# The shortest chunk of tokens first, and the attention statistics in the order of the tokens

## The chip, the cores and the metric

The kernel runs on one core of one Trainium2 chip. The metric is the device time of one launch in microseconds (us). The engines of the core are TensorE (PE, matrix products and transposes), VectorE (DVE), ScalarE (ACT), GpSimd (POOL), and SyncE (SP), which here only issues DMAs.

## The reference

One decoder layer for 1024 tokens of a prompt and 8 single tokens of other sequences, all in fp32. What matters here:

```python
h = rms_norm(x, norm_mix_pre)
q, k, v, u, gates = jnp.split(h @ w_in, IN_SPLITS, axis=-1)
...
# three groups of 4 heads, each with its own dilation (1, 4, 16); one log-sum-exp per token, head, group
w = jax.nn.softmax(jnp.stack(lses, axis=0), axis=0)
o = jnp.einsum('gbth,gbthd->bthd', w, jnp.stack(outs, axis=0))
...
a, gte = jnp.split(u, 2, axis=-1)
z = a * jax.nn.sigmoid(gte)        # then a causal depthwise convolution of width 31, and so on
```

Behind them come the merge of both branches, the output projection, a SwiGLU feed-forward and a per-layer embedding, each with an RMSNorm. The change doesn't touch these.

## The kernel before

The 1032 tokens are the free axis of all activations, features lie on the 128 partitions, so a tensor of 1024 features is 8 pieces of 128 x 1032. For matmuls the tokens go in three chunks, `CH`: 0 to 383, 384 to 767, and 768 to 1031 (264 tokens, the 8 single ones among them). Every fp32 product is done as three matmuls on split operands (L278 to L280): high weight by high activation, high weight by low activation, low weight by high activation. `hh` and `hl` are the high and low parts of the normed input, `wh` and `wl` those of a weight of 8 x 128 x 128, whose raw form (`raw`) is loaded from DRAM, split by ACT (`wh`) and by DVE (`wl`). `gemm_bank` computes one bank of PSUM: 8 pieces of k, so 24 matmuls, for one weight and one chunk.

`first_pairs` is the start of the program. Nothing is normed yet, so the first two chunks that it takes are multiplied unnormed ("plain"), each token's factor being applied later to the product (`u_evac` multiplies by `rbx`, sigmoid, multiplies again; `a_evac` multiplies into `z`). Meanwhile the factors are made: `norm_sums` squares on ACT and adds on DVE (tiles `sq`, `acc`), `token_rstd` transposes the sums on PE (L325), reduces on DVE (`cs`), and raises to the power -1/2 on POOL (`r`); `bcast_cols` spreads the factor back over the partitions with three transposes on PE (L337). The third chunk is normed properly before it is multiplied (`norm_apply`: a scaling `hf` on DVE, `hh` on ACT, `hl` on DVE, for each of 8 pieces), and the first two are normed afterwards for all later weights. Each engine takes its work in order; what the order is, is decided when the program is built, by a scheduler that mostly keeps the written order of `first_pairs` on ACT and DVE but lets PE's banks run in turn.

Attention runs in the order that suits each group's dilation. Each (token, head, group) has two statistics (maximum and sum), collected in `stats[g]` (tiles `st`) by blocks of the group's order. `stats_by_tokens(g)` writes them over DRAM (`d_st`) and reads them back so that partition and column are a token's, with POOL issuing the DMAs. From them `combine` makes one factor for each token, head and group, sends it to DRAM and reads it broadcast over 64 partitions (`fb`), and multiplies the groups' outputs (`ogl`, 128 x 1024, two heads of a group) by it: three multiplies and two adds for each of two pairs of heads, all on DVE, between other work (the feed-forward has not begun; the norm of the convolution and its products run on PE, and other sums of squares, tiles `acc` and `sq`, stand on DVE and ACT).

Of the kernel before, what the change touches and what calls it, by code (L numbers as in the profile page):

```python
# [12 lines left out]
AF = mybir.ActivationFunctionType  # L13
# [3 lines left out]
P = 128  # L17
S = 1024
# [3 lines left out]
KT = D // P  # L22
# [5 lines left out]
CH = ((0, 384), (384, 384), (768, 264))  # L28
CW = 384
# [29 lines left out]
def decoder_step(ctx: ExitStack, tc: tile.TileContext, ins, outs):  # L59
# [30 lines left out]
    def rl(s):  # L90
        return rlp.tile([P, CW], F32, tag="rl", name=nm(s))
# [332 lines left out]
    xin = {}  # L424

    def vec(v, f):
        return vecs[:, v, f:f + 1]

    def load_x(c):
        xin[c] = chunk_slots("xin")  # L430
        load_chunk(xin[c][0], xT_in, c)

    hs = [(act("hh", F32R), act("hl", F32R)) for _ in range(KT)]
    rbx = [rl("rb0"), rl("rb1")]

    def load_raw(n):
        while w_emitted[0] < n:
# [7 lines left out]

    def norm_factor(r1, c):
        rb = bcast_cols(r1, c)
        A.activation(rbx[c], rb[:, :CW], AF.Copy)

    def norm_apply(c, fs, rb):  # L450
        t0, n = CH[c]
# [10 lines left out]
            last = (hf, f)  # L462

    def norm_plain(c, f):
        split_scaled(xin[c][1][f], vec(V_MIXPRE, f), hs[f][0], hs[f][1], c)


    def setup():
# [115 lines left out]

    def stats_by_tokens(g):

        dst, src = stats[g], d_st[g]
        G.dma_start(src, stats[g])
        if g == 0:
            for b in range(8):  # L590
                G.dma_start(dst[b * 16:(b + 1) * 16], src[:, b].rearrange("(p b) n -> p b n", b=8))
        elif g == 1:
            for l in range(2):
                for e in range(2):
                    G.dma_start(dst[l * 64:(l + 1) * 64, e * 4:(e + 1) * 4],
                                 src[e::2, l::2])
        else:
            for j in range(2):
                for i in range(2):
                    G.dma_start(dst[j::2, i * 4:(i + 1) * 4],  # L600
                                 src[i * 64:(i + 1) * 64, j * 4:(j + 1) * 4])

    class Unit:

# [152 lines left out]
    def triple_bank(i, j, c):  # L757
        g, hp = triples[i]
        t0, n = CH[c]
        if c == 0:  # L760
# [110 lines left out]
    def combine(beside):  # L871
# [48 lines left out]
        for _ in range(W2):  # L920
            yield next(beside)
        for hp in range(2):
            ovs = [o[:, :S].rearrange("p (t b) -> p b t", b=8) for o in o3]
            for g in range(3):
                V.tensor_mul(ovs[g], ovs[g], f3[g][:, :S].rearrange("p (b t) -> p b t", b=8))
                yield 1.2
                if g:
                    V.tensor_add(o3[0][:, :S], o3[0][:, :S], o3[g][:, :S])
                    yield 1.2
            V.tensor_copy(o3[0][:, S:T], osm[:, hp])  # L930
            o = o3[0]
# [15 lines left out]
    def u_evac(i, c, sig, ps, rb=None):  # L947
        n = CH[c][1]
        s = rl("sg")
        if rb is not None:  # L950
            V.tensor_mul(s, ps[:, :n], rb)
            A.activation(s, s, AF.Sigmoid)
            V.tensor_mul(s, s, rb)
        else:
            A.activation(s[:, :n], ps[:, :n], AF.Sigmoid)
        sig[i, c] = s

    def a_evac(i, c, sig, zs, ps):
        t0, n = CH[c]
        if c == 0:  # L960
# [6 lines left out]
        if c < 2:  # L967
            return
        V.tensor_mul(t38, ps[:, 226:264], s[:, 226:264])
# [32 lines left out]
    def first_pairs():  # L1002

        nonlocal gtags, mtags
        mtags, gtags = deque(MT0), deque(GT0)
        sig, zs = {}, {}  # L1010
        pinned[0] = True
        A.activation(mhalf2, mhalf, AF.Sigmoid)
        xin[0] = chunk_slots("xin")
        SY.dma_start(vecs, ins["vecs"])
        load_chunk(xin[0][0][:1], xT_in, 0)
        load_raw(1)
        load_chunk(xin[0][0], xT_in, 0, 1)
        load_raw(3)
        load_x(1)
        for f in range(2):  # L1020
            norm_plain(0, f)
        ensure(0)
        for f in range(2, KT):
            norm_plain(0, f)
        g0 = gemm_bank(wi_gate[0], hs, 0)
        load_raw(4)
        load_x(2)
        SY.dma_start(cc, ins["cc"])
        SY.dma_start(taps, ins["taps"])
        ensure(2)  # L1030
        a0 = gemm_bank(wi_a[0], hs, 0)
        t = norm_sums(0)
        for f in range(3):
            norm_plain(1, f)
        r1 = token_rstd(t, 0)
        ensure(3)
        for f in range(3, 6):
            norm_plain(1, f)
        g1 = gemm_bank(wi_gate[1], hs, 0, mid=lambda: norm_factor(r1, 0), at=KT - 1)
        u_evac(0, 0, sig, g0, rbx[0])  # L1040
        a_evac(0, 0, sig, zs, a0)
        for f in range(6, KT):
            norm_plain(1, f)
        t = norm_sums(1)
        u_evac(1, 0, sig, g1, rbx[0])
        a1 = gemm_bank(wi_a[1], hs, 0)
        r1 = token_rstd(t, 1)
        t = norm_sums(2)
        a_evac(1, 0, sig, zs, a1)
        g0 = gemm_bank(wi_gate[0], hs, 1, mid=lambda: norm_factor(r1, 1))  # L1050
        r2 = token_rstd(t, 2)
        u_evac(0, 1, sig, g0, rbx[1])
        rb = []
        a0 = gemm_bank(wi_a[0], hs, 1, mid=lambda: rb.append(bcast_cols(r2, 2)))
        norm_apply(2, range(2), rb[0])
        a_evac(0, 1, sig, zs, a0)
        g1 = gemm_bank(wi_gate[1], hs, 1)
        norm_apply(2, range(2, KT), rb[0])
        u_evac(1, 1, sig, g1, rbx[1])
        a1 = gemm_bank(wi_a[1], hs, 1)  # L1060
        norm_apply(0, range(3), rbx[0])
        a_evac(1, 1, sig, zs, a1)
        ensure(4)
        for i in range(2):
            u_evac(i, 2, sig, gemm_bank(wi_gate[i], hs, 2))
            norm_apply(0, range(3 + 3 * i, 6 + 2 * i), rbx[0])
            a_evac(i, 2, sig, zs, gemm_bank(wi_a[i], hs, 2))
            ensure(wi_a[1] + 2 + i)
        norm_apply(1, range(KT), rbx[1])
        xin.clear()  # L1070
        pinned[0] = False
        mtags, gtags = deque(["m"]), deque(["g"])

    def triple(i):
        for j in range(3):
            for c in (0, 2, 1) if i == 0 and j == 0 else range(3):
# [584 lines left out]
```

## Time and profile before

| | before |
|---|---|
| median of 3 runs | 1696.8 us (1696.02 to 1697.6) |
| profiled execution, its own time | 1694.75 us |
| its span in the trace | 1693.0 us |
| PE busy | 1675.4 us (99% of the span) |
| DVE busy | 1201.1 us (71%) |
| ACT busy | 610.6 us (36%) |
| granted TensorE clock, mean | 1.00 |

The span is the time from the first to the last instruction of the profiled execution; the run's own time has 1.75 us more around it. Times of single instructions below come from this one execution. Matmuls are pipelined, so the busy time of one in a row is longer than the distance to the next.

### The profile page before, as it was taken

The page shows a single profiled execution, that of the slowest core. Times are in us where ns is not written, and L with a number is a line of the kernel's source. Part 1 is how long each engine was busy: PE and PEld are TensorE (multiplying, and loading weights), DVE is VectorE, ACT ScalarE, POOL GpSimd, SP SyncE. Part 2 cuts the span into 40 slices and gives each one's busy share as a digit, 9 for nine tenths or more (in the row PEclk, how much of TensorE's full clock was granted, in tenths as well). Part 3 has the DMA queues.
Part 4 walks back from the last instruction along what each step waited for, and adds up shares of the span by engine and source line. Part 5 has one row for each costly group of instructions (what it writes and reads, how often), then busy time and mean ns, then how long its engine had stood idle before and what let it go on. Part 6 is the DMA issues. An engine that isn't in the chain of part 4 may idle for free.

```text
span 1693.0 us, 28665 instructions
## 1 busy us (share of the span) xinstructions
PE 1675.4 (99%) x11651; PEld 1648.9 (97%) x11651; DVE 1201.1 (71%) x2084; ACT 610.6 (36%) x1231; POOL 29.2 (2%) x46
## 2 busy tenths in 40 slices
PE   8999999999999999999999999999999999999999
PEld 7999999999999999999999999999999999999998
DVE  7899879958979686553679666666666445548863
ACT  6434435444343345123444323323323311213520
POOL 1000010000000000000000000000000000000000
PEclk9999999999999999999999999999999999999999
DMA  5242121121354364423232222323333523420411
GB/s 191 65 125 66 44 69 57 50 82 51 102 177 159 93 191 128 147 73 120 85 124 82 81 99 88 101 86 114 110 107 125 185 109 114 162 96 14 159 51 47
DMA packets 81307, 174.72 MB, mean 103 GB/s; under 512 B 11491, under 2 KB 50291, under 8 KB 80791
## 3 DMA queue, kind: packets, MB, share of 16 engines
q1 hardware_dynamic: 80566, 172.69, 31.2%
q8 instruction: 91, 1.49, 0.4%
q0 software_dynamic: 608, 0.20, 0.1%
q14 instruction: 42, 0.34, 0.1%
HBM read 136.20 MB, written 50.16 MB: 110 GB/s over the span
## 4 chain that ended last, share of the span: by engine, by line
PE 91%; DVE 5%; issue 1%; ACT 1%; DMA 1%; POOL 0%; SPq 0%; POOLq 0%; DVEq 0%; ACTq 0%
PE g L278 29%; PE g L280 29%; PE g L279 29%; DVE y L120 3%; PE O L677 1%; PE S L632 1%; PE PT L659 1%; DVE wl L120 1%; DVE ogl L120 0%; DVE acc L120 0%; PE m L337 0%; DMA res<-d_x 0%; PE m L325 0%; POOL r L120 0%; DMA raw<-in_w_in_dram 0%
## 5 line engine op out<-in xcount | busy, mean ns | idle before, releaser
L278 PE MATMUL g<-hh,wh 128*128 128x384 f32 (+1 forms) x1200 | 392.9, 327 | 7.1 <-ACT wh L120 7.1
L280 PE MATMUL g<-hh,wl 128*128 128x384 f32 (+1 forms) x1200 | 384.2, 320 | 0.2 <-DVE wl L120 0.2
L279 PE MATMUL g<-hl,wh 128*128 128x384 f32 (+1 forms) x1200 | 383.7, 320 | 0.0
L120 DVE SCALAR_TENSOR_TENSOR y<-z,taps,y 128x1023 f32<-128x1023 f32 (+14 forms) x240 | 303.9, 1267 | 36.7 <-ACT y L120 31.1
L278 PEld LDWEIGHTS g<-hh,wh 128*128 128x128 f32 x1200 | 226.4, 189 | 14.4 <-ACT wh L120 7.0
L279 PEld LDWEIGHTS g<-hl,wh 128*128 128x128 f32 x1200 | 226.2, 188 | 0.6 <-DVE hl L120 0.3
L280 PEld LDWEIGHTS g<-hh,wl 128*128 128x128 f32 x1200 | 225.7, 188 | 0.8 <-DVE wl L120 0.8
L280 PE MATMUL g<-uh,wl 128*128 128x344 f32 x528 | 168.7, 320 | 0.0
L279 PE MATMUL g<-ul,wh 128*128 128x344 f32 x528 | 168.5, 320 | 0.0
L278 PE MATMUL g<-uh,wh 128*128 128x344 f32 x528 | 163.1, 321 | 0.6 <-DVE fa L120 0.6
L120 DVE TENSOR_TENSOR wl<-raw,wh 128x1024 fp32r<-128x1024 f32 x106 | 129.1, 1221 | 35.3 <-ACT wh L120 28.6
L120 DVE TENSOR_TENSOR pk<-pk,g 128x258 f32<-128x258 f32 x266 | 105.4, 420 | 55.0 <-PE g L280 39.0
L120 ACT ACTIVATE wh<-raw 128x1024 fp32r<-128x1024 f32 x106 | 110.7, 1051 | 6.9 <-PE g L279 3.8
L278 PE MATMUL g<-mh,wh 128*128 128x344 f32 x336 | 107.3, 322 | 0.0
L280 PE MATMUL g<-mh,wl 128*128 128x344 f32 x336 | 107.1, 320 | 0.0
L279 PE MATMUL g<-ml,wh 128*128 128x344 f32 x336 | 107.0, 320 | 0.0
L120 DVE TENSOR_TENSOR fa<-fa,g 128x344 f32<-128x344 f32 x96 | 47.1, 510 | 77.2 <-PE g L280 76.8
L279 PEld LDWEIGHTS g<-ul,wh 128*128 128x128 f32 x528 | 99.3, 188 | 0.0
L280 PEld LDWEIGHTS g<-uh,wl 128*128 128x128 f32 x528 | 99.2, 188 | 0.0
L278 PEld LDWEIGHTS g<-uh,wh 128*128 128x128 f32 x528 | 98.0, 188 | 0.9 <-DVE fa L120 0.9
L278 PE MATMUL g<-th,wbh 128*128 128x258 f32 x304 | 86.0, 283 | 0.0
L280 PE MATMUL g<-th,wbl 128*128 128x258 f32 x304 | 85.9, 283 | 0.0
(234 smaller groups left out, 3700.3 us busy)
## 6 DMA issues: line engine op xcount, KB each, us to landing
raw<-in_w_in_dram SPq DMA_DIRECT2D x50, 512.0 KB
raw<-in_w_ffn_in_dram SPq DMA_DIRECT2D x44, 512.0 KB
hr<-d_h SPq DMA_DIRECT2D x22, 516.0 KB
raw<-in_w_ffn_out_dram SPq DMA_DIRECT2D x22, 512.0 KB
d_h<-pk SPq DMA_DIRECT2D x38, 258.0 KB
out_kvs_dram<-in_cache_kv_w_dram SPq DMA_DIRECT2D x16, 510.0 KB
d_x<-mo SPq DMA_DIRECT2D x24, 172.0 KB
out_yT_dram<-fa SPq DMA_DIRECT2D x24, 172.0 KB
```

The lines of the kernel that those rows point to most:

```text
L120: ins = fn(*a, **k)
L278: TE.matmul(ps, hi_w, xh, start=first, stop=False)
L279: TE.matmul(ps, hi_w, xl, start=False, stop=False)
L280: TE.matmul(ps, lo_w, xh, start=False, stop=last)
L632: TE.matmul(sp[h][:, o:o + nk], qT[h * 64:(h + 1) * 64, blk * P:(blk + 1) * P], kT[h * 64:(h + 1) * 64, (blk + 1) * P - nk:(blk + 1) * P], ...
L659: TE.transpose(ps[:, o:o + P], e[:, o:o + P], ident)
L677: TE.matmul(ps[h * 64:(h + 1) * 64, i * P:(i + 1) * P], vtok[:, k0:k0 + 64], self.p[half][:, o:o + P], start=kb == kbs[0], stop=kb == kbs[-1])
```

## The change

Three things are changed. First, `first_pairs` takes the chunks in another order: the chunk of 264 tokens first, then tokens 0 to 383, both plain, and tokens 384 to 767 last, with the norm ahead of the product; the factors `rbx` are now kept for chunks 2 and 0 and sliced to the chunk's width, and the transposes that end a pair of `z` run when its third chunk is done, whichever that is. Second, `stats_by_tokens` no longer turns the statistics into an order of 8 successive tokens on a partition: group 0 is left as it is, groups 1 and 2 are written to DRAM in two permuting DMAs (pieces of 32 and of 128 bytes) so that a row is a token, and read back by one DMA in blocks of 128 tokens. Third, the factor `fb` comes out in the tokens' order, so the multiplies in `combine` need no view that permutes. The first triple's first weight takes its chunks in the order 2, 1, 0 instead of 0, 2, 1.

```diff
-    rbx = [rl("rb0"), rl("rb1")]
+    rbx = {0: rl("rb0"), 2: rl("rb2")}
...
     def stats_by_tokens(g):
 
-        dst, src = stats[g], d_st[g]
-        G.dma_start(src, stats[g])
         if g == 0:
-            for b in range(8):
-                G.dma_start(dst[b * 16:(b + 1) * 16], src[:, b].rearrange("(p b) n -> p b n", b=8))
-        elif g == 1:
+            return
+
+        rows = d_st[g].rearrange("p b n -> (p b) n")
+        if g == 1:
+            to = rows.rearrange("(l i r) n -> l i r n", l=2, r=4)
             for l in range(2):
-                for e in range(2):
-                    G.dma_start(dst[l * 64:(l + 1) * 64, e * 4:(e + 1) * 4],
-                                 src[e::2, l::2])
+                G.dma_start(to[l], stats[1][:, l::2])
         else:
-            for j in range(2):
-                for i in range(2):
-                    G.dma_start(dst[j::2, i * 4:(i + 1) * 4],
-                                 src[i * 64:(i + 1) * 64, j * 4:(j + 1) * 4])
+            to = rows.rearrange("(l j i r) n -> i l j r n", j=2, i=2, r=4)
+            for i in range(2):
+                G.dma_start(to[i], stats[2][i * 64:(i + 1) * 64].rearrange("p (j r) n -> p j r n", j=2))
+        G.dma_start(stats[g], rows.rearrange("(b p) n -> p b n", p=P))
...
         for hp in range(2):
-            ovs = [o[:, :S].rearrange("p (t b) -> p b t", b=8) for o in o3]
             for g in range(3):
-                V.tensor_mul(ovs[g], ovs[g], f3[g][:, :S].rearrange("p (b t) -> p b t", b=8))
+                V.tensor_mul(o3[g][:, :S], o3[g][:, :S], f3[g][:, :S])
                 yield 1.2
...
+        CA, CB, CC = 2, 0, 1
...
-        load_chunk(xin[0][0][:1], xT_in, 0)
+        load_chunk(xin[CA][0][:1], xT_in, CA)
         load_raw(1)
-        load_chunk(xin[0][0], xT_in, 0, 1)
+        load_chunk(xin[CA][0], xT_in, CA, 1)
         load_raw(3)
-        load_x(1)
+        load_x(CB)
...
-        g1 = gemm_bank(wi_gate[1], hs, 0, mid=lambda: norm_factor(r1, 0), at=KT - 1)
-        u_evac(0, 0, sig, g0, rbx[0])
-        a_evac(0, 0, sig, zs, a0)
+        g1 = gemm_bank(wi_gate[1], hs, CA, mid=lambda: norm_factor(r1, CA), at=KT - 1)
+        u_evac(0, CA, sig, g0, rbx[CA])
+        a_evac(0, CA, sig, zs, a0)
...
-            u_evac(i, 2, sig, gemm_bank(wi_gate[i], hs, 2))
-            norm_apply(0, range(3 + 3 * i, 6 + 2 * i), rbx[0])
-            a_evac(i, 2, sig, zs, gemm_bank(wi_a[i], hs, 2))
+            u_evac(i, CC, sig, gemm_bank(wi_gate[i], hs, CC))
+            norm_apply(CA, range(3 + 3 * i, 6 + 2 * i), rbx[CA])
+            a_evac(i, CC, sig, zs, gemm_bank(wi_a[i], hs, CC))
             ensure(wi_a[1] + 2 + i)
-        norm_apply(1, range(KT), rbx[1])
+        norm_apply(CB, range(KT), rbx[CB])
```

On PE, around the first factor (the transposes L337 into `m_320`), the program before has these rows; `g_298` is the third bank, of the third weight, on the first chunk, and the end of a name counts the buffers.

```order
L278 MATMUL g_298<-hh_122,wh_218 128x384
L279 MATMUL g_298<-hl_123,wh_218 128x384
L280 MATMUL g_298<-hh_122,wl_219 128x384
L278 MATMUL g_298<-hh_124,wh_218 128x384
L279 MATMUL g_298<-hl_125,wh_218 128x384
L280 MATMUL g_298<-hh_124,wl_219 128x384
L337 MATMUL m_320<-ident,r_55_284 128x128 x3
L278 MATMUL g_298<-hh_126,wh_218 128x384
L279 MATMUL g_298<-hl_127,wh_218 128x384
```

After the change PE has at this place, where `g_367` is the fourth bank of the first chunk and `g_429` the first bank of the second chunk:

```order
L278 MATMUL g_298<-hh_126,wh_218 128x264
L279 MATMUL g_298<-hl_127,wh_218 128x264
L280 MATMUL g_298<-hh_126,wl_219 128x264
L278 MATMUL g_367<-hh_112,wh_288 128x264
L279 MATMUL g_367<-hl_113,wh_288 128x264
L337 MATMUL m_320<-ident,r_55_284 128x128 x3
L278 MATMUL g_429<-hh_112,wh_159 128x384
L279 MATMUL g_429<-hl_113,wh_159 128x384
L280 MATMUL g_429<-hh_112,wl_160 128x384
L278 MATMUL g_429<-hh_114,wh_159 128x384
L280 MATMUL g_367<-hh_112,wl_289 128x264
```

The factor's transposes moved behind the end of the third bank and two matmuls of the fourth: ahead of them stood 69 matmuls of 384 columns, and stand 74 of 264.

Also on PE, early in the third chunk of the start, the program before runs straight through its first bank (`g_606`):

```order
L280 MATMUL g_606<-hh_116,wl_160 128x264
L278 MATMUL g_606<-hh_118,wh_159 128x264
L279 MATMUL g_606<-hl_119,wh_159 128x264
L280 MATMUL g_606<-hh_118,wl_160 128x264
L278 MATMUL g_606<-hh_120,wh_159 128x264
L279 MATMUL g_606<-hl_121,wh_159 128x264
```

After the change the third chunk's first two banks (`g_608` and `g_647`) take turns there:

```order
L278 MATMUL g_608<-hh_118,wh_159 128x384
L278 MATMUL g_647<-hh_112,wh_212 128x384
L279 MATMUL g_647<-hl_113,wh_212 128x384
L280 MATMUL g_647<-hh_112,wl_213 128x384
L279 MATMUL g_608<-hl_119,wh_159 128x384
L280 MATMUL g_608<-hh_118,wl_160 128x384
L278 MATMUL g_608<-hh_120,wh_159 128x384
L278 MATMUL g_647<-hh_114,wh_212 128x384
```

The pieces of the chunk's norm (`hl_119`, `hl_121` and so on) are thus read at every sixth matmul there, where they were read at every third. The last piece, `hl_127`, is read by the 35th matmul on the chunk.

On DVE, in the combine, the rows stand in the same places; the two multiplies (`ogl<-ogl,fb`) have another shape. Before:

```order
L120 TENSOR_TENSOR acc_5747<-acc_5747,sq_5758 128x384
L120 TENSOR_TENSOR ogl_5550<-ogl_5550,fb_5797 128x8x128
L120 TENSOR_TENSOR acc_5747<-acc_5747,sq_5790 128x384
L120 TENSOR_TENSOR acc_5747<-acc_5747,sq_5794 128x384
L120 TENSOR_TENSOR acc_5747<-acc_5747,sq_5807 128x384
L120 TENSOR_TENSOR ogl_5551<-ogl_5551,fb_5798 128x8x128
L120 TENSOR_TENSOR acc_5747<-acc_5747,sq_5811 128x384
```

After the change:

```order
L120 TENSOR_TENSOR acc_5734<-acc_5734,sq_5745 128x384
L120 TENSOR_TENSOR ogl_5537<-ogl_5537,fb_5784 128x1024
L120 TENSOR_TENSOR acc_5734<-acc_5734,sq_5777 128x384
L120 TENSOR_TENSOR acc_5734<-acc_5734,sq_5781 128x384
L120 TENSOR_TENSOR acc_5734<-acc_5734,sq_5794 128x384
L120 TENSOR_TENSOR ogl_5538<-ogl_5538,fb_5785 128x1024
L120 TENSOR_TENSOR acc_5734<-acc_5734,sq_5798 128x384
```

Nothing moved here: one run of 1024 elements has taken the place of 8 by 128 in another order.

## Rows read from the trace of the kernel before

**Rows 1.** The page, part 1: busy time, share of the span, instructions.
```profile
PE 1675.4 (99%) x11651; PEld 1648.9 (97%) x11651; DVE 1201.1 (71%) x2084; ACT 610.6 (36%) x1231; POOL 29.2 (2%) x46
```
**Rows 2.** Waits of PE: line, releaser: us, times, longest.
```profile
PE g L278 <- ACT wh L120: 7.1, 1, 7.1
PE m L337 <- POOL r L120: 2.3, 3, 0.9
PE m L325 <- DVE acc L120: 2.2, 2, 1.4
```
**Rows 3.** Tile `ogl`: ns min/median/max, first and last start.
```profile
L120 DVE TENSOR_TENSOR ogl<-ogl,fb x6: 2211/2262/2312, 581.1 to 614.6; 128x1024 f32<-128x1024 f32 x6
L120 DVE TENSOR_TENSOR ogl<-ogl,ogl x4: 1207/1242/1270, 590.3 to 616.9; 128x1024 f32<-128x1024 f32 x4
```
**Rows 4.** Timeline, 578 to 590: start, us, engine, operation, [idle before, releaser].
```profile
582.54 1.76 ACT L120 ACTIVATE sq<-y 128x384 f32<-128x384 f32 x4
583.26 1.90 DVE L120 TENSOR_TENSOR acc<-acc,sq 128x384 f32<-128x384 f32 x3
...
585.08 2.21 DVE L120 TENSOR_TENSOR ogl<-ogl,fb 128x1024 f32<-128x1024 f32 x1
...
587.82 0.55 PE L325 MATMUL m<-ident,acc 128*128 128x128 f32 x3 [1.42 <-DVE acc L120]
```
**Rows 5.** Timeline, 608 to 632.
```profile
610.22 2.25 DVE L120 TENSOR_TENSOR ogl<-ogl,fb 128x1024 f32<-128x1024 f32 x1
...
628.65 2.04 DVE L120 TENSOR_TENSOR acc<-acc,sq 128x264 f32<-128x264 f32 x4
...
629.66 0.34 PE L280 MATMUL g<-hh,wl 128*128 128x384 f32 x1
...
630.75 0.55 PE L325 MATMUL m<-ident,acc 128*128 128x128 f32 x3 [0.75 <-DVE acc L120]
```
**Rows 6.** Timeline, 46 to 63, PE: first matmuls of the third chunk and behind.
```profile
46.31 0.28 PE L278 MATMUL g<-hh,wh 128*128 128x264 f32 x1
...
58.12 0.34 PE L278 MATMUL g<-hh,wh 128*128 128x384 f32 x1
...
62.33 0.27 PE L973 MATMUL m<-ident,t 128*38 128x128 f32 x1
```
**Rows 7.** Timeline, 4 to 24: the first factor's chain.
```profile
11.67 1.06 ACT L120 ACTIVATE wh<-raw 128x1024 fp32r<-128x1024 f32 x1 [0.21 <-DMA raw<-in_w_in_dram]
...
14.01 2.90 DVE L120 TENSOR_TENSOR acc<-acc,sq 128x384 f32<-128x384 f32 x6
...
19.96 1.78 POOL L120 TENSOR_TENSOR r<-r,mhalf 128x3 f32<-128x3 f32 x1 [18.65 <-DVE r L120]
...
21.80 0.54 PE L337 MATMUL m<-ident,r 128*128 128x128 f32 x3
```
**Rows 8.** Windows, 4 to 8: us, engines' busy time, clock, DMA share, GB/s.
```profile
4.00:8.00 4.00, 0.95 (x2) 0.50 (x2) 2.12 (x3) 3.17 (x5) 0.00 (x0) 1.00 1.02 382
```
**Rows 9.** Timeline, 22 to 50: second and third factor.
```profile
30.51 0.49 PE L325 MATMUL m<-ident,acc 128*128 128x128 f32 x3
...
32.05 0.77 DVE L120 TENSOR_TENSOR acc<-acc,sq 128x264 f32<-128x264 f32 x2
...
33.24 0.54 PE L337 MATMUL m<-ident,r 128*128 128x128 f32 x3
...
36.05 0.49 PE L325 MATMUL m<-ident,acc 128*128 128x128 f32 x3
...
38.45 0.54 PE L337 MATMUL m<-ident,r 128*128 128x128 f32 x3 [0.87 <-POOL r L120]
```
**Rows 10.** Timeline, 44 to 47, DVE: the third chunk's last splits.
```profile
45.19 1.01 DVE L120 TENSOR_TENSOR hl<-hf,hh 128x264 fp32r<-128x264 f32 x2
```
**Rows 11.** Timeline, 470 to 530: the last group's reads and the first use.
```profile
472.82 2.14 POOL L120 DMA_DIRECT2D st<-d_st  x4 [1.46 <-DMA d_st<-st]
...
528.50 0.18 DVE L120 TENSOR_TENSOR stt<-st,st 128x32 f32<-128x32 f32 x1
```

More of the change, by code (lines that the diff above doesn't have):

```diff
@@ L447, in norm_factor @@
         rb = bcast_cols(r1, c)
-        A.activation(rbx[c], rb[:, :CW], AF.Copy)
+        n = CH[c][1]
+        A.activation(rbx[c][:, :n], rb[:, :n], AF.Copy)
     def norm_apply(c, fs, rb):
@@ L464, in norm_plain @@
     def norm_plain(c, f):
-        split_scaled(xin[c][1][f], vec(V_MIXPRE, f), hs[f][0], hs[f][1], c)
+        split_scaled(xin[c][1][f][:, :CH[c][1]], vec(V_MIXPRE, f), hs[f][0], hs[f][1], c)
     def setup():
@@ L759, in triple_bank @@
         t0, n = CH[c]
-        if c == 0:
+        if c == (2 if i == 0 and j == 0 else 0):
             held[j] = act("qkv"[j] + "T")
@@ L950, in u_evac @@
         if rb is not None:
-            V.tensor_mul(s, ps[:, :n], rb)
-            A.activation(s, s, AF.Sigmoid)
-            V.tensor_mul(s, s, rb)
+            V.tensor_mul(s[:, :n], ps[:, :n], rb[:, :n])
+            A.activation(s[:, :n], s[:, :n], AF.Sigmoid)
+            V.tensor_mul(s[:, :n], s[:, :n], rb[:, :n])
         else:
@@ L956, in u_evac @@
         sig[i, c] = s
+    evacs = {}
     def a_evac(i, c, sig, zs, ps):
         t0, n = CH[c]
-        if c == 0:
+        if i not in zs:
             z = act("z")
@@ L966, in a_evac @@
         V.tensor_mul(z[:, t0:t0 + npr], ps[:, :npr], s[:, :npr])
-        if c < 2:
+        if c == 2:
+            V.tensor_mul(t38, ps[:, 226:264], s[:, 226:264])
+        evacs[i] = evacs.get(i, 0) + 1
+        if evacs[i] < 3:
             return
-        V.tensor_mul(t38, ps[:, 226:264], s[:, 226:264])
         def rows():
@@ L1012, in first_pairs @@
         A.activation(mhalf2, mhalf, AF.Sigmoid)
-        xin[0] = chunk_slots("xin")
+        xin[CA] = chunk_slots("xin")
         SY.dma_start(vecs, ins["vecs"])
-        load_chunk(xin[0][0][:1], xT_in, 0)
+        load_chunk(xin[CA][0][:1], xT_in, CA)
         load_raw(1)
-        load_chunk(xin[0][0], xT_in, 0, 1)
+        load_chunk(xin[CA][0], xT_in, CA, 1)
         load_raw(3)
-        load_x(1)
+        load_x(CB)
         for f in range(2):
-            norm_plain(0, f)
+            norm_plain(CA, f)
         ensure(0)
         for f in range(2, KT):
-            norm_plain(0, f)
-        g0 = gemm_bank(wi_gate[0], hs, 0)
+            norm_plain(CA, f)
+        g0 = gemm_bank(wi_gate[0], hs, CA)
         load_raw(4)
-        load_x(2)
+        load_x(CC)
         SY.dma_start(cc, ins["cc"])
@@ L1030, in first_pairs @@
         ensure(2)
-        a0 = gemm_bank(wi_a[0], hs, 0)
-        t = norm_sums(0)
+        a0 = gemm_bank(wi_a[0], hs, CA)
+        t = norm_sums(CA)
         for f in range(3):
-            norm_plain(1, f)
-        r1 = token_rstd(t, 0)
+            norm_plain(CB, f)
+        r1 = token_rstd(t, CA)
         ensure(3)
         for f in range(3, 6):
-            norm_plain(1, f)
-        g1 = gemm_bank(wi_gate[1], hs, 0, mid=lambda: norm_factor(r1, 0), at=KT - 1)
-        u_evac(0, 0, sig, g0, rbx[0])
@@ L1041, in first_pairs @@
-        a_evac(0, 0, sig, zs, a0)
+            norm_plain(CB, f)
+        g1 = gemm_bank(wi_gate[1], hs, CA, mid=lambda: norm_factor(r1, CA), at=KT - 1)
+        u_evac(0, CA, sig, g0, rbx[CA])
+        a_evac(0, CA, sig, zs, a0)
         for f in range(6, KT):
[L1043 to L1050, printed above, removed]
@@ L1051, in first_pairs @@
-        r2 = token_rstd(t, 2)
-        u_evac(0, 1, sig, g0, rbx[1])
-        rb = []
[L1054 to L1062, printed above, removed]
+            norm_plain(CB, f)
@@ new lines, in first_pairs @@
+        t = norm_sums(CB)
+        u_evac(1, CA, sig, g1, rbx[CA])
+        a1 = gemm_bank(wi_a[1], hs, CA)
+        r1 = token_rstd(t, CB)
+        t = norm_sums(CC)
+        a_evac(1, CA, sig, zs, a1)
+        g0 = gemm_bank(wi_gate[0], hs, CB, mid=lambda: norm_factor(r1, CB))
+        r2 = token_rstd(t, CC)
+        u_evac(0, CB, sig, g0, rbx[CB])
+        rb = []
+        a0 = gemm_bank(wi_a[0], hs, CB, mid=lambda: rb.append(bcast_cols(r2, CC)))
+        norm_apply(CC, range(2), rb[0])
+        a_evac(0, CB, sig, zs, a0)
@@ L1063, in first_pairs @@
+        g1 = gemm_bank(wi_gate[1], hs, CB)
+        norm_apply(CC, range(2, KT), rb[0])
+        u_evac(1, CB, sig, g1, rbx[CB])
+        a1 = gemm_bank(wi_a[1], hs, CB)
+        norm_apply(CA, range(3), rbx[CA])
+        a_evac(1, CB, sig, zs, a1)
         ensure(4)
         for i in range(2):
-            u_evac(i, 2, sig, gemm_bank(wi_gate[i], hs, 2))
-            norm_apply(0, range(3 + 3 * i, 6 + 2 * i), rbx[0])
-            a_evac(i, 2, sig, zs, gemm_bank(wi_a[i], hs, 2))
+            u_evac(i, CC, sig, gemm_bank(wi_gate[i], hs, CC))
+            norm_apply(CA, range(3 + 3 * i, 6 + 2 * i), rbx[CA])
+            a_evac(i, CC, sig, zs, gemm_bank(wi_a[i], hs, CC))
@@ L1075, in triple @@
         for j in range(3):
-            for c in (0, 2, 1) if i == 0 and j == 0 else range(3):
+            for c in (2, 1, 0) if i == 0 and j == 0 else range(3):
                 ensure(wi_qkv[i, j] + 1)
```

## The prediction

> **What bounds the kernel now.** I read the page's busy times first: TensorE (PE) is busy for 1675.4 of the 1693.0 us, VectorE (DVE) for 71%, ScalarE (ACT) for 36%, GpSimd (POOL) for 2% [rows 1]. So time moves only where PE waits, or where it gets more or slower matmuls; the change leaves their number and their columns alone and only reorders them. Next I read PE's waits: 7.1 us for the first split weight, three waits for POOL's factor (2.3 in sum), two for DVE's sums of squares (2.2) [rows 2]. The changed places touch all three: the start decides when the first weight and the factors come, and the combine's multiplies stand on DVE ahead of sums of squares. Past the first weight, which comes from a load, 4.5 us are at stake, under 0.3% of the span.
>
> **The combine.** Six multiplies of 128x1024, whose view takes the elements in another order, have a median of 2262 ns; the adds of the same tiles, shape and type, without a view, have 1242 ns [rows 3]. My estimate for the changed multiply is the add's time: 1.02 us less each, 6.1 less on DVE. DVE isn't the bound, so what counts is the two waits behind it.
>
> *First wait.* PE's transposes at 587.82 waited 1.42 us for a sum of squares. Ahead of its last add two multiplies stand on DVE, the first of the six (at 581.1) and the one at 585.08; three adds at 583.26 stand between [rows 3, 4]. Shortening the first frees only little: the adds' squares come from ACT, four in 1.76 us from 582.54, so the first is there at 582.98 and the adds begin 0.28 sooner at best. Shortening the second frees its full 1.02, as it stands directly ahead of the last add. Together 1.3 by these rows; the adds then run close behind the squares (one each 0.44), so I take 1.2. Bounds: 0 if the time isn't the view's, and 1.4, the wait.
>
> *Second wait.* The transposes at 630.75 started 1.09 after the matmul before them, where such matmuls lie 0.175 apart [rows 5, 6], so 0.9 is lost. They waited for DVE's four adds from 628.65. Ahead on DVE are the last two multiplies, at 610.22 and 614.6 [rows 3, 5]. Two times 1.02 is more than 0.9, so the wait goes: 0.9, bounds 0 and 0.9. Sum of the combine: **-2.1**, bounds 0 and -2.3.
>
> One rule speaks against this. The Trainium skill (VectorE: DVE Perf Modes, "Mode 1× (REGULAR) — the baseline") says that the base mode gives one result per cycle for fp32 and for odd strides alike. By it the view would cost nothing and this part would be worth 0; the rows of this case differ by 1.8 times at one shape and type, though the operator differs too, so I go by the rows.
>
> **The start.** PE's pitch is 0.123 us for a matmul of 264 columns (96 from 46.31 to 58.12) and 0.175 for 384 (24 from 58.12 to 62.33) [rows 6]. With the work only reordered, what can change is PE's lateness: the time less the pitches of all matmuls done. Three factors make PE wait, and I follow them; how many matmuls stand ahead of each is counted in the order of both programs.
>
> *First factor.* Its chain before: the third weight's split on ACT at 11.67, which waited for its load; DVE's six adds from 14.01 in 2.90, one more add, three splits of the next chunk; POOL's power at 19.96; PE at 21.80 [rows 7]. Ahead of that weight stand the four loads of the first chunk, each now 2 x 128 x 120 x 4 = 122,880 bytes smaller: at 382 GB/s [rows 8] 0.32 us, so 1.3 for the four. Seven adds of 264 take 0.385 each, as the pair at 32.05 [rows 9], where those of 384 took 0.483: 0.7 for the seven. The three splits stay 384 wide. So PE gets the factor at 21.80 - 2.0 = 19.8. But ahead of it there is less to do: before 69 matmuls of 384 and three transposes (0.25), 12.3 us in all, lateness 9.5; after 74 of 264, 9.35 us in all, lateness 10.45. PE with the lateness of before would be there at 18.8, so it waits 1 us or more, and the lateness is +0.95.
>
> *Third factor.* Behind the first, the new order has 22 matmuls of 264 and 35 of 384 up to the next sums' transposes: 19.8 + 0.27 + 2.7 + 6.1 = 28.9. From such transposes to the factor took 2.40 (36.05 to 38.45) or 2.73 (30.51 to 33.24) [rows 9]; new, ten matmuls stand between, 1.75, so PE waits again: second factor at 31.3. Then 19 matmuls of 384 with the factor's 0.27, 3.6, and again 2.40: third at 37.3. Work ahead of it is 149 x 0.175 = 26.1 before (38.45, lateness 12.35) and 96 x 0.123 + 70 x 0.175 = 24.05 after (lateness 13.25): +0.9. The chain with 2.73 gives +1.2 for it; I go by the lower, since the gates of the first chunk, which stand ahead of that chain on DVE, are now narrower: **+0.9**. Bounds: -0.1, if the first factor is there at 18.8 (then all three are 1.0 sooner); +1.5, if the four loads give only half of the 1.3.
>
> *What is normed last.* The last chunk is now 384 wide. Before, DVE's last pair of splits ended at 45.19 + 1.01 = 46.2 [rows 10], 7.75 after the factor, and PE began on this chunk at 46.31 [rows 6]. With 384 columns, the sixteen steps on DVE (a scaling and a split for each of eight pieces) grow, as the adds did by 0.10 for the same columns [rows 7, 9]; I allow 0.125 each: ready at 37.3 + 7.75 + 2.0 = 47.05. PE enters the chunk 26 matmuls behind the factor and, since the order now takes two banks in turn there, reads the last split as its 35th matmul: 37.3 + 0.27 + 60 x 0.175 = 48.1. That is 1.0 of margin, so 0; its loss is bounded below with the rivals.
>
> **The statistics.** Nineteen DMA issues on POOL become six, and group 0's go. POOL is busy for 2%, and only the other groups' reads stand behind them. The last group's reads were issued at 472.82, the first use is at 528.50 [rows 11]: over 50 us of cover, so 0. Without the cover it would be the 1.46 that POOL waited for the write and the 2.14 of the reads' issue, 3.6.
> The Trainium skill (DMA: Bandwidth & Descriptors, "Specifications") says that transfers under 512 bytes are done as read-modify-write, which speaks against the new writes in pieces of 32 and 128 bytes. Were they ten times as slow as those of before, they would still lie under the cover, so the sum stays.
>
> **Sum.** -2.1 + 0.9 = -1.2. The profiled execution took 1694.75 us, 1.75 over its span, and is 2.05 below the median of 1696.8 (runs from 1696.02 to 1697.6). So 1693.55 for such an execution, and **1695.6** for the median. About 0.2%, 3.4 us, is what a measurement of this kernel can tell from no change.
>
> **Rivals.**
> - The combine pays half: ACT's squares, not DVE, set the adds' end [rows 4]; 0.6 and 0.45 gained: 1696.8 - 1.05 + 0.9 = 1696.65. Against it: the second multiply has only one add behind it.
> - The start gains a little, its lower bound: 1696.8 - 2.1 - 0.1 = 1694.6. For it: ACT's work ahead of the weights gets shorter too.
> - The multiply stays at 2.26 us: 1696.8 + 0.9 = 1697.7. Against it: [rows 3]. This mechanism is the rule on VectorE above.
> - Slower: the third chunk's norm comes late. DVE makes a piece in about 1.0 us (two steps like those of [rows 10]) where PE can ask for one each three matmuls, 0.52; if PE stands on the chunk before DVE is ahead enough, it waits at each of the eight pieces, 4 us at most: 1699.6. It sets in when the last piece is more than 1.0 late against 47.05, and decides the sign at 2.2 late. For it: PE's first matmul on the chunk came only 0.1 after the last split, and the chunk grows by 45%. Against it: the two banks in turn.
> - The statistics come late: 1695.6 + 3.6 = 1699.2. Against it: [rows 11].
>
> **Chances.** Forecast 0.55, half 0.12, the start gains 0.13, multiply unchanged 0.05, norm late 0.08, statistics 0.02, something unseen 0.05. The runs before lie 0.8 to each side of their median, and that lies on all of them. The range goes from 1693.5 (the start gains, and 1.1 below it) to 1697.4 (half, and 0.85 above); the last four cases lie mostly outside. Faster by over 3.4 us needs 2.2 us more than the forecast, more than the bounds of both terms give: 0.08, for the unseen and the runs' spread. Slower by over 3.4 is the worse end of the norm case and the unseen: 0.06. The rest is within, 0.86.
>
> **What would show it.** The multiplies at about 1.24 us in the tile's groups; PE's waits for sums of squares gone or under 0.3 us each; a wait of 1 us or more for POOL's factor near 19.8, and waits at the two others that stay; none for the third chunk's split between 42 and 49; none for the statistics near 528. I would be wrong if the multiplies keep their time, if a split of the third chunk releases PE, or if the freed time on DVE moves a later transfer or a buffer that PE then waits for.

## The result, and the profile after

The changed kernel takes 1698.81 us in the median of 20 runs (1696.86 to 1701.49), the kernel before beside it 1696.33 (1695.55 to 1697.91): a ratio of 1.0015, 95% interval 1.0009 to 1.0021. It is slower by 2.5 us, where 1695.6 was forecast and 1697.4 was the upper end of the range. That it is slower is clear; 2.5 us are 0.15%, less than the 0.2% that the forecast called a change.

The profiled execution after took 1697.24 us and that of before 1694.75; both lie 1.6 under their medians, so the two traces differ by the same 2.5 us. What made some runs after longer still is not in this trace; that of e8, below, shows it. PE's waits in it (line, releaser: us, times, longest):

```profile
PE g L278 <- ACT wh L120: 6.7, 1, 6.7
PE m L337 <- POOL r L120: 4.0, 5, 1.5
PE m L480 <- DMA strow<-in_state_conv_dram: 2.3, 1, 2.3
PE m L325 <- DVE acc L120: 0.2, 1, 0.2
```

Against [rows 2] the waits for the sums of squares are nearly gone (0.2 for 2.2), those for POOL's factors have grown (4.0 for 2.3), and a wait that the kernel before didn't have stands first among the new: 2.3 us for `strow`, the rows of the convolution's state, which are loaded from DRAM and transposed on PE behind the start. Tile `ogl` after, with [rows 3] for before:

```profile
L120 DVE TENSOR_TENSOR ogl<-ogl,fb x6: 1216/1218/1221, 584.8 to 616.2; 128x1024 f32<-128x1024 f32 x6
L120 DVE TENSOR_TENSOR ogl<-ogl,ogl x4: 1214/1220/1225, 593.0 to 617.5; 128x1024 f32<-128x1024 f32 x4
```

The multiplies went from 2262 to 1218 ns and now take what the adds take. The timeline at the two old waits, which answers to [rows 4, 5]:

```profile
588.70 1.22 DVE L120 TENSOR_TENSOR ogl<-ogl,fb 128x1024 f32<-128x1024 f32 x1
...
590.44 0.55 PE L325 MATMUL m<-ident,acc 128*128 128x128 f32 x3 [0.25 <-DVE acc L120]
...
632.58 0.49 PE L325 MATMUL m<-ident,acc 128*128 128x128 f32 x3
```

And the start, which answers to [rows 7, 9]: the third weight's split, the sums, the first factor's power, the three factors on PE.

```profile
11.16 1.06 ACT L120 ACTIVATE wh<-raw 128x1024 fp32r<-128x1024 f32 x1 [0.30 <-DMA raw<-in_w_in_dram]
...
13.40 2.14 DVE L120 TENSOR_TENSOR acc<-acc,sq 128x264 f32<-128x264 f32 x6
...
20.18 0.54 PE L337 MATMUL m<-ident,r 128*128 128x128 f32 x3 [1.46 <-POOL r L120]
...
31.85 0.54 PE L337 MATMUL m<-ident,r 128*128 128x128 f32 x3 [0.28 <-POOL r L120]
...
37.97 0.54 PE L337 MATMUL m<-ident,r 128*128 128x128 f32 x3 [0.86 <-POOL r L120]
```

Now the two traces can be laid over each other, matmul by matmul, from the transposes of the state on, behind which both programs do the same in the same order. Before, the last twelve of these transposes and the last matmul of all stand at

```profile
68.69 1.40 PE L479 MATMUL m<-ident,strow 120*128 120x120 f32 x12
...
1688.57 0.32 PE L280 MATMUL g<-pTh,wl 128*128 128x344 f32 x1
```

and after they stand at

```profile
69.77 0.60 PE L480 MATMUL m<-ident,strow 120*128 120x120 f32 x4 [2.32 <-DMA strow<-in_state_conv_dram]
...
72.48 1.40 PE L480 MATMUL m<-ident,strow 120*128 120x120 f32 x12
...
1690.28 0.32 PE L280 MATMUL g<-pTh,wl 128*128 128x344 f32 x1
```

So PE is 3.79 us late at the transposes. It is 2.62 late at the first old wait (587.82 became 590.44), 1.83 at the second (630.75 became 632.58), and 1.71 at its last matmul. The combine gave back 1.96, near the forecast 2.1. The start lost 3.79, not 0.9: about 2.5 of it at the wait for the state, 1.3 ahead of it. Another 0.4 us is lost behind PE's last matmul (1693.0 - 1688.57 before, 1695.1 - 1690.28 after), and 0.4 outside the span (1.75 before, 2.14 after). From the start of PE's last matmul to the end of the run's own time that makes 6.2 us before and 7.0 after.

**Where the state's wait comes from.** The part of the critical chain from 59 us on (start, us, what):

```profile
60.38 1.24 DVE wl L120
61.62 0.02 issue
61.63 0.36 SPq L120
62.00 0.05 issue
62.05 7.58 DMA strow<-in_state_conv_dram
69.63 0.14 issue
69.77 0.60 PE m L480 x4
```

SP's queue around it, in the kernel before and then after:

```profile
58.95 0.37 SPq L120 DMA_DIRECT2D raw<-in_w_in_dram  x1
59.37 0.41 SPq L120 DMA_DIRECT2D strow<-in_state_conv_dram  x1
...
63.92 0.34 SPq L120 DMA_DIRECT2D strow<-in_state_conv_dram  x1
64.36 0.96 SPq L120 DMA_DIRECT2D raw<-in_w_in_dram  x1
```

```profile
58.15 3.85 SPq L120 DMA_DIRECT2D raw<-in_w_in_dram  x2
62.05 0.43 SPq L120 DMA_DIRECT2D strow<-in_state_conv_dram  x1
...
64.95 0.34 SPq L120 DMA_DIRECT2D strow<-in_state_conv_dram  x1
```

Before, one weight's load is issued, then the state's first half; the next weight, the tenth, comes behind the second half. After, the tenth weight's load stands ahead of both halves. Its buffer is free only when DVE has split an earlier weight (60.38 + 1.23), and SP waits for that; SP's waits between 57 and 63 us after the change:

```profile
SPq L120 <- DVE wl L120: 3.0, 1, 3.0
```

So the state's first half is issued 2.7 us later (62.05 for 59.37) and then shares the transfers with 512 KB of weight, while PE comes to its transposes at about 67.3. The trace also keeps sixteen marks for each load, one for each part of it that has landed. Before, the last mark of the first half stands at 64.88, of the second at 68.08: 1.0 and 0.6 us ahead of the transposes at 65.90 and 68.69. After, the first half takes 7.58 us from issue to landing where it took 5.51, so of the 4.75 us that it lands later (69.63 for 64.88) 2.7 are the issue and 2.1 the transfer. Fifteen of its marks stand by 67.81 and one at 69.63, so most of PE's wait is for a single part; e2 and e8 show the same (69.91 behind 68.03, 70.28 behind 68.25). Why that part comes so late stays open. The diff shows no such move. The program's order does, in one row on SP:

```
before                                            after
DMA raw_746<-in_w_in_dram 128x1024                DMA raw_746<-in_w_in_dram 128x1024
DMA strow_818<-in_state_conv_dram 120x1024        DMA raw_1049<-in_w_in_dram 128x1024
DMA out_cvp_dram<-zrow_813 30x128                 DMA strow_819<-in_state_conv_dram 120x1024
DMA out_cvs_dram<-zrow_813 8x128                  DMA out_cvp_dram<-zrow_813 30x128
DMA strow_819<-in_state_conv_dram 120x1024        DMA out_cvs_dram<-zrow_813 8x128
DMA raw_1049<-in_w_in_dram 128x1024               DMA strow_820<-in_state_conv_dram 120x1024
```

### The profile page after: what moved, and what is told of

Same layout as the page of the kernel before. It is cut to its first block, busy times and chain, and to the rows that moved or that the text cites. A ratio compares the mean times of both kernels' runs of the same rounds, so it can differ in the third digit from the quotient of the medians.

```text
span 1695.1 us, 28642 instructions
## 1 busy us (share of the span) xinstructions
PE 1675.7 (99%) x11651; PEld 1649.5 (97%) x11651; DVE 1194.0 (70%) x2084; ACT 609.6 (36%) x1231; POOL 23.3 (1%) x33
## 3 DMA queue, kind: packets, MB, share of 16 engines
q8 instruction: 91, 1.49, 0.4%
## 4 chain that ended last, share of the span: by engine, by line
PE 91%; DVE 4%; DMA 1%; ACT 1%; issue 1%; POOL 0%; SPq 0%; POOLq 0%; DVEq 0%; ACTq 0%
PE g L278 29%; PE g L280 29%; PE g L279 29%; DVE y L120 3%; PE O L676 1%; PE S L631 1%; PE PT L658 1%; DVE wl L120 1%; DMA strow<-in_state_conv_dram 0%; DMA raw<-in_w_in_dram 0%; PE m L337 0%; DMA res<-d_x 0%; PE m L325 0%; POOL r L120 0%; ACT wh L120 0%
```

## Experiments

The theory after the result: the combine gives 2 us; the start costs 1.3 by its factors and 2.5 by the state's wait, and the wait can cost more, because the runs of the changed kernel are spread over 4.6 us, and of the twelve over 1698 us eleven list a granted clock of 0.997 to 0.999, of the eight shorter ones three (0.999). The rivals: the loss is the statistics' DMAs or the combine's; the state is late since the whole start is late, not since SP waits; the spread has nothing to do with the wait. Ratios are to the kernel before on the same chip; e1 to e4 ran on one chip, e5 to e8 on a second, e9 and e10 on a third.

**e1_combine_only.** The old start with `stats_by_tokens` and `combine` of the changed kernel:

```diff
-            ovs = [o[:, :S].rearrange("p (t b) -> p b t", b=8) for o in o3]
             for g in range(3):
-                V.tensor_mul(ovs[g], ovs[g], f3[g][:, :S].rearrange("p (b t) -> p b t", b=8))
+                V.tensor_mul(o3[g][:, :S], o3[g][:, :S], f3[g][:, :S])
```

> The statistics and the multiplies of the changed kernel, on the start of the kernel before. Theory (the multiplies shorten two waits of PE, and the late loads of the convolution's state belong to the start): both waits for sums of squares go, 1.2 and 0.8 to 0.9 us, so 2.0 under the kernel before, about 1694.3 against 1696.3, and no wait of PE for the state's rows. Rival (the changed kernel's loss comes from the statistics' DMAs or from the tail): this one is slower than before, by 1 us or more.

Measured: 1694.41 us against 1695.88, ratio 0.9992 (0.9983 to 1.0001). The sign and the place are the theory's (the interval just reaches no change), the size is 1.5 and not 2.0. So the statistics' part is not where the loss is. It has a small price all the same, about as much as the missing 0.5: from the start of PE's last matmul to the end of the run's own time it is 6.2 us in the profiled runs with the old statistics and multiplies (before, e2, e4), and 6.7 to 7.0 in the nine with the new ones, 6.7 here. Which of the two does it, and how, stays open. PE also waited 0.5 us for the state in this run's trace, where the theory had none, though its start is that of before: there, too, the load lands close to its use.

**e2_start_only.** The reverse: the new start, with the old statistics and the strided multiplies.

```diff
+            for g in range(3):
+                V.tensor_mul(ovs[g], ovs[g], f3[g][:, :S].rearrange("p (b t) -> p b t", b=8))
-                V.tensor_mul(o3[g][:, :S], o3[g][:, :S], f3[g][:, :S])
```

> The new order of the chunks, with the statistics and the strided multiplies of the kernel before. Theory: start +1.3 us by the factors and +2.5 us or more by the wait for the convolution's state, nothing back from the combine: 1700 to 1701 against 1696.3, with the runs spread over 3 us or more as in the changed kernel. Rival (the two parts hang together, or the loss is the combine's): within 1 us of the kernel before.

Measured: 1699.73 against 1695.88, ratio 1.0022 (1.0013 to 1.0031), runs from 1698.18 to 1702.64. The start alone costs 3.85 us, and with the combine's -1.5 that makes 2.4, the changed kernel's 2.5. The parts add up.

**e3_state_first.** The changed kernel, with only SP's order put back, by an edge (an order added to the program: this DMA is issued behind those two):

```diff
         for i in range(2):
-            SY.dma_start(strow[i][:120, :D], ...)
+            dm = SY.dma_start(strow[i][:120, :D], ...)
+        held["state"] = dm.ins
...
-        SY.dma_start(r[:, :n * P].rearrange("p (k m) -> p k m", m=P), src)
+        with tc.issue_after(held["state"]) if j == 9 else nullcontext():
+            SY.dma_start(r[:, :n * P].rearrange("p (k m) -> p k m", m=P), src)
```

> The changed kernel with one edge more on SP's queue: the load of the tenth weight is issued behind both loads of the convolution's state, as in the kernel before. Theory (that weight's load, moved ahead of them, made PE wait for the state and in some runs cost clock after it): PE's wait of 2.3 us goes, the runs stand within 1 us of each other, the median is 1695.6 to 1696 (+1.3 of the start, -2.0 of the combine), 3 us under the changed kernel. Rival (the state is late since the whole start is late, or the spread is not from there): less than 1 us under the changed kernel, spread as wide.

Measured: 1695.89 against 1695.88, ratio 1.0000 (0.9991 to 1.0009), runs from 1695.22 to 1696.79. One edge on SP takes back the whole loss and the spread with it (1.6 us wide where the changed kernel had 4.6; that one wasn't timed on this chip); with the load's new place the planner (the scheduler that orders the program) also took the first four transposes up to 1 us ahead on PE. PE still waits for the state's second half, which stands behind other DMAs on SP as it did before:

```profile
PE m L482 <- DMA strow<-in_state_conv_dram: 0.7, 1, 0.7
```

**e4_state_late.** The kernel before, with the tenth weight's load put ahead of both loads of the state (`load_raw(10)` ahead of them, and an edge on each to it).

> The kernel before with one edge more on SP's queue: both loads of the convolution's state are issued behind the load of the tenth weight. Theory: PE waits for the state by 2 to 5 us, as it waited not at all before, the time is 1698.5 to 1702 with runs more spread than before, and the granted clock of the longer runs is under 1.00. Rival (the queue's order doesn't matter, since the data rate and not the place decides): within 0.7 us of the kernel before.

Measured: 1696.51 against 1695.88, ratio 1.0005 (0.9996 to 1.0013), runs from 1694.79 to 1699.14. The theory's number fell: PE's wait is 0.2 us. The trace says why this is no clean test. With the loads late in the program, the planner also put their transposes later on PE:

```profile
69.19 0.58 PE L483 MATMUL m<-ident,strow 120*128 120x120 f32 x4
...
71.01 1.45 PE L483 MATMUL m<-ident,strow 120*128 120x120 f32 x12 [0.19 <-DMA strow<-in_state_conv_dram]
```

They stood at 65.90 and 68.69 before. The spread did come, as the theory had it: the runs lie over 4.4 us, and the longest (1699.14) lists a granted clock of 0.999; its cause isn't in this trace, which is of one of the shorter runs. What is left of it: a late load costs little where its use is late too; in the changed kernel the load was moved and the use wasn't moved far enough.

**e5_state_early.** The changed kernel with both loads of the state some 45 us earlier on SP, and nothing else changed in SP's order:

```diff
+        held["strow"] = [act("strow") for _ in range(2)]
+        for i in range(2):
+            SY.dma_start(held["strow"][i][:120, :D], ...)
         norm_apply(CC, range(2, KT), rb[0])
```

> The changed kernel with both loads of the convolution's state issued some 30 us earlier on SP, ahead of the seventh weight, so that no weight's wait for its buffer stands ahead of them. Theory (the whole loss beyond the factors is the state's lateness; 0.7 us of it were left with the order of before): no wait of PE for the state, 0.7 us under the kernel that only had its queue order back, so 0.6 to 0.8 under the kernel before. Rival (the remaining loss of that kernel against the combine alone is all of the factors' start): as that kernel, within 0.3 us of the kernel before.

Measured: 1695.04 against 1695.63, ratio 0.9997 (0.9988 to 1.0005). The loads are issued at 16.98, and the planner puts their transposes 26 rows earlier on PE; the tenth weight's load still waits as long for its buffer (3.0 us), and PE waits for the state no more:

```profile
PE g L278 <- ACT wh L120: 6.7, 1, 6.7
PE m L337 <- POOL r L120: 3.2, 5, 0.9
PE g L278 <- DVE fa L120: 0.6, 1, 0.6
PE g L280 <- DVE wl L120: 0.5, 1, 0.5
PE m L325 <- DVE acc L120: 0.2, 1, 0.2
```

0.6 under the kernel before is the number that the theory gave; the rival's (no difference) lies in the interval too, so that e5 is faster than e3 is shown by the trace (the wait is gone) and not by the times.

**e6_combine_state_early.** e1 with the loads of the state early, by the same edit: the old order of the chunks and all else that helps.

> The start of the kernel before, the statistics and multiplies of the changed one, and the state's loads early as in the run above. Theory: the 0.5 us that PE still waited for the state with the combine alone goes too: 0.4 to 0.6 under that run, so 2.0 under the kernel before. Rival (the wait comes back elsewhere, since the loads now meet others): no better than the combine alone, 1.5 under the kernel before.

Measured: 1693.74 against 1695.63, ratio 0.9990 (0.9981 to 0.9999): 1.9 us under the kernel before, faster than both kernels of this case. Beside e5 on the same chip, which differs from it by the order of the chunks alone, it is 1.3 us faster in the medians. That is the price of the new order, and it is what the traces of before and after gave (1.3); the traces of e5 and e6 themselves differ by 0.5 in their spans, since e5's is of the shortest of its runs.

**e7_factor_first.** e5, with the sums' reduction ahead of the splits of the second chunk on DVE:

```diff
-        for f in range(3):
-            norm_plain(CB, f)
         r1 = token_rstd(t, CA)
         ensure(3)
-        for f in range(3, 6):
+        for f in range(6):
             norm_plain(CB, f)
```

> The changed kernel with the state's loads early and with the first factor's chain freed: on DVE the sums' reduction stands ahead of the six splits of the second chunk, three of which stood ahead of it. Theory (PE waits for the first factor since its chain is late, 1.0 to 1.5 us): the factor comes at about 18.7 us in place of 20.2, its wait shrinks to under 0.9 while five fewer matmuls stand ahead of it, so 0.9 us under the same kernel with the splits ahead. Rival (the second and third factor's chains take it back, since each is as long): within 0.4 us of it.

Measured: 1694.87 against 1695.63, ratio 0.9997 (0.9988 to 1.0006), 0.2 under e5: the rival's number, but by another mechanism. The first factor didn't come earlier at all. In e7:

```profile
17.15 0.49 PE L325 MATMUL m<-ident,acc 128*128 128x128 f32 x3
...
17.68 0.56 DVE L120 TENSOR_REDUCE cs<-m 128x3 f32<-128x384 f32 x1 [1.49 <-PE m L325]
...
20.36 0.54 PE L337 MATMUL m<-ident,r 128*128 128x128 f32 x3 [1.25 <-POOL r L120]
```

From the sums' transposes to the factor takes 3.21 us, as in the kernel before (18.59 to 21.80) and in e5 (16.40 to 19.61), with DVE's splits ahead or not. In e7 DVE waited 1.49 us for these transposes: PE, at their place among its matmuls, was the late end of the chain. In the traces of before and of e5 the transposes and DVE's three splits end within 0.1 us of each other, so taking the splits away could gain nothing there. In the first trace of the changed kernel the same stretch is 4.03 (16.15 to 20.18), and DVE was the late end, by 0.8; which one is late differs from run to run.

**e8_changed_again.** The changed kernel once more, beside e5 to e7.

> The changed kernel as it is, beside the others on this chip. Theory: 2.5 to 3 us over the kernel before, the runs over a width of 4 us, and the longer of them with the lower granted clock. Rival (its time was the chip's of that day): within 1 us of the kernel before.

Measured: 1698.79 against 1695.63, ratio 1.0018 (1.0009 to 1.0028). Three runs took 1696.14 to 1696.83, seven 1698.59 to 1699.59. The profiled execution is one of the seven (1699.46), and shows what the trace of the first one (1697.24) didn't. Windows of it (us, busy time of PE, PEld, DVE, ACT, POOL, granted clock, DMA share, GB/s):

```profile
66.00:67.60 1.60, 1.60 (x10) 1.40 (x9) 1.60 (x5) 1.08 (x3) 0.00 (x0) 1.00 1.00 214
67.60:70.30 2.70, 0.13 (x1) 0.00 (x0) 2.70 (x6) 1.66 (x4) 0.00 (x0) 1.00 0.51 123
...
71.00:72.00 1.00, 1.00 (x6) 1.00 (x5) 0.16 (x1) 0.00 (x0) 0.00 (x0) 0.56 0.00 0
72.00:73.00 1.00, 1.00 (x5) 1.00 (x4) 0.00 (x0) 0.00 (x0) 0.00 (x0) 0.50 0.00 0
73.00:74.00 1.00, 1.00 (x5) 1.00 (x4) 0.00 (x0) 0.00 (x0) 0.00 (x0) 0.50 0.00 0
74.00:75.00 1.00, 1.00 (x8) 0.97 (x7) 0.00 (x0) 0.00 (x0) 0.00 (x0) 0.73 0.00 0
```

PE stood idle for 2.7 us, and from about 71 us, when it had begun again, its granted clock fell from 1.00 to 0.50, from 2.4 to 1.2 GHz, until past 74 us. The matmuls of 384 columns there lie 0.32 us apart in place of 0.175:

```profile
71.28 0.52 PE L279 MATMUL g<-hl,wh 128*128 128x384 f32 x1
71.60 0.52 PE L280 MATMUL g<-hh,wl 128*128 128x384 f32 x1
71.92 0.52 PE L278 MATMUL g<-hh,wh 128*128 128x384 f32 x1
```

Some eleven of them at 0.145 us more each are 1.6 us, which come on top of the wait itself. The trace of e2 has the fall too (0.81 between 69 and 70 us, while PE still stood in its wait of 2.4, and 0.50 until 73). The first trace of the changed kernel has a wait of 2.3 without the fall, and e3 (a wait of 0.7), e5 and e6 have no fall. That all seven longer runs of e8 have it is likely but not shown, as only one of them has a trace. Beside e8 on the same chip e5, which moves only the state's loads, is 3.75 us faster, and no run of one lies among those of the other: that is what the loads' place cost, wait and clock together.

**e9_power_warm and e10_combine_warm.** e5 and e6, each with one more power on POOL at the start, of three columns of ones, whose result nobody reads:

```diff
+        one, warm = (colp.tile([P, 3], F32, tag=t, name=t, bufs=1) for t in ("one", "warm"))
+        V.memset(one, 1.0)
+        G.tensor_tensor(warm, one, mhalf[:, :3], op=ALU.pow)
```

> The changed kernel with the state's loads early, and a power of three columns of ones on POOL at the start of the program, whose result nobody reads; in the traces POOL's first power took 1.78 us and the two others 0.85 to 1.02. Theory (the first call of that operation is the long one, and the new start is exposed to it, since PE waits for the first factor): the first factor's power takes about 0.9 us, the wait for it shrinks by 0.8 us, and the time is 0.6 to 0.9 us under the same kernel without it, so 1.2 to 1.5 under the kernel before. Rival (DVE's splits and not POOL's power end the chain last, or the second and third chain take it back as they did when DVE's splits were moved): within 0.3 us of the same kernel without it.

> The start of the kernel before, the statistics and multiplies of the changed one, the state's loads early, and the same power of ones at the start. Theory: the start of before waits only 0.3 us for the first factor, so the gain is 0.3 at most, 2.0 to 2.2 us under the kernel before, and the fastest of all. Rival (the long first power sits on the path there too): 0.7 us or more under the same kernel without it, 2.6 under the kernel before.

Measured: e9 1694.79 against 1696.18, ratio 0.9994 (0.9985 to 1.0002); e10 1693.96 against 1696.18, ratio 0.9988 (0.9979 to 0.9997). The mechanism of the theory fell. In e9's trace the first factor's power is as long as it was:

```profile
1.29 0.87 POOL L120 TENSOR_TENSOR warm<-one,mhalf 128x3 f32<-128x3 f32 x1
18.39 1.77 POOL L120 TENSOR_TENSOR r<-r,mhalf 128x3 f32<-128x3 f32 x1 [16.23 <-DVE r L120]
30.79 1.02 POOL L120 TENSOR_TENSOR r<-r,mhalf 128x3 f32<-128x3 f32 x1 [10.63 <-DVE r L120]
37.06 0.85 POOL L120 TENSOR_TENSOR r<-r,mhalf 128x3 f32<-128x3 f32 x1 [5.25 <-DVE r L120]
```

An earlier call doesn't shorten it. Why the first is twice as long as the others stays open; e9 and e10 differ from e5 and e6 by no more than the intervals allow.

## Why the prediction was wrong

**The combine** was right by its mechanism and nearly by its size: 1.04 us less for each multiply (1.02 forecast), 1.17 and 0.79 at the two waits (1.2 and 0.9) in the traces of before and after. The rule of the Trainium skill that I had kept as a rival (VectorE: DVE Perf Modes, "Mode 1× (REGULAR) — the baseline": odd strides run at the base rate in fp32) doesn't hold here: the same operation on the same tiles takes 2262 ns with the view and 1218 without. In timed runs the part, with the statistics, is worth 1.5 (e1).

**The start's factors** had the right sign and about the right size: +0.9 forecast, +1.3 in the traces and between e5 and e6, inside the bounds of -0.1 to +1.5. The 0.4 between them is less than traces of one start differ by: the third factor came at 38.45 to 39.59 in five traces of the old order, that of before being the earliest, and at 37.35 to 38.26 in six of the new (e7, whose order differs, left out). One term was off in most traces, the first factor's "1.3 for the four loads". After the change the third weight was split at 11.16 and not at 11.67, so 0.5 earlier: the transfers ran at 326 GB/s between 4 and 8 us, where I had taken the 382 of before. In six of the seven traces of the new order it was 11.16 to 11.46, and 10.52 in e5, whose transfers ran at 374; there the first factor came at 19.61 and the third at 37.35, as forecast (19.8 and 37.3). The seven adds gave 0.9 (2.52 us from 13.40 to the three splits, 3.41 before) and not 0.7. In the first trace after, the factor came at 20.18. The chain also left out PE's own transposes of the sums, which e7 shows as the late end once the splits are gone.

**What is normed last** cost nothing, as forecast: no wait of PE for the third chunk's split. **The statistics** cost nothing on the path either: their last read is issued at 477.42 and used at 532.28. The 0 in the sum was too low all the same: 0.5 to 0.8 us behind PE's last matmul go with the new statistics and multiplies in every profiled run, and the cover at their use says nothing of that.

**The step that failed** is the one that isn't there. The change was costed by what it does on PE, DVE, ACT and POOL, and for SP by the bytes of the first loads alone. That one weight's load had moved ahead of the state's loads on SP stood in the program's order and was given no price. "Three factors make PE wait, and I follow them" left out what stood behind the third: the state's transposes, whose load a list of waits doesn't show, since a wait that is just not there leaves no row. Before, the transposes at 65.90 and 68.69 found their data landed 1.0 and 0.6 us earlier (e1, with the same start, waited 0.5 us for it). With the load moved, the first half landed 4.75 us later, 2.7 by its issue and 2.1 by its transfer, and PE waited 2.3; in e8 the clock's fall cost 1.6 more. Shown by experiments: SP's order is the cause (e3 undoes it and gets 2.5 to 3 us back, e5 takes the loads out of its way and is 3.75 us faster than e8 on its chip). Argued only: that the transfer is longer because of the 512 KB directly ahead.

Of the rivals none was this one. The rival on the other side, the third chunk's late norm, had 0.08 of the chances and didn't happen; the sentence that a freed engine might move a later transfer that PE then waits for named the kind, but gave it no row and no time.

## What to carry to other kernels

Where a change lets a planner order the program anew, compare every queue row by row, the DMA queue first, and give each moved transfer a price: what its issue waits for (a buffer, 3.0 us here), who stands behind it, and how close to its use that one lands. A wait list shows only loads that are late already; those that are just in time have to be looked up by their issue and their first use. A short stop of PE can cost more than its length, since the clock may fall with it: 2.7 us of waiting took 1.6 more in e8.

## What the runs showed of the hardware

- A multiply of 128 x 1024 in fp32 took 2262 ns with the tile that it reads and writes viewed as 8 by 128 in another order (the factor is read as it lies) and 1218 ns without. The Trainium skill (SBUF — State Buffer, "Door 1: The DMA port swizzle") says that SBUF has lines of 16 bytes and that accesses that leave a line at each step pay for it; that fits, as the view steps by 8 elements of 4 bytes, but no run here tries other steps.
- The granted clock fell from 1.00 to 0.50 behind 2.7 us without matmuls in e8 and at the end of 2.4 us without them in e2, and stayed at 1.00 over 2.3 us without them in the first trace of e8's program. The Trainium skill (TensorE: Matmul & The Clock Gate, "What's actually happening") says that the full clock is granted for activity and withdrawn when PE idles; the traces of e2 and e8 agree.
- The moment from which PE first runs at full pace differs from trace to trace by some 2 us. The first matmuls of 384 columns have a busy time of 0.52 or 0.53 us, as at a granted clock of 0.50 in e8, and then of 0.34, as at 1.00; the profile's granted clock reads 1.00 over both, so it doesn't show this rise. The first with 0.34 stood at 10.94 us in the trace of before and at 13.07 in that of e1, whose start is the same program, and the first sums' transposes at 18.59 and 19.69. So single traces of one program differ by 1 us here ahead of all that the change touches, which is as much as the terms of the sum.
